# Moving low-part subtractions from DMA to VectorE, and re-spacing background taps, in a one-core hybrid trunk layer

## The chip, the core and the metric

The kernel runs on one core of one Trainium2 chip. The metric is the device time of one execution in microseconds (us). The core's engines run side by side, each through its own list of instructions in a fixed order, and they wait for one another by semaphores: PE (TensorE, the matrix unit; PEld is its weight load), DVE (VectorE), ACT (ScalarE), POOL (GpSimd, which here mostly issues DMAs) and SP (SyncE, which issues the loads and stores).

## The reference, cut to what matters

One layer over 512 prompt tokens and 64 sample tokens (T = 576 in all), model width 1024. A normed input goes through one wide projection and feeds three branches; sigmoid gates merge them, and a last projection closes the layer.

```python
h = _rmsnorm(x, norm_pre_w)
glu_v, glu_g, conv_gate, z, xbc, dt_raw, q, xa_gate, gates = jnp.split(h @ w_in, points, axis=-1)
u = glu_v * jax.nn.sigmoid(glu_g)
c, new_a = _causal_dwconv(u, st_a, conv_dw_w, conv_dw_b)              # width 31
c = jax.nn.silu(_layernorm(c, conv_ln_w, conv_ln_b)) * jax.nn.silu(conv_gate)
out_a = c @ conv_out_w
...                                                                  # y: state-space mixer
out_b = y @ ssd_out_w
...                                                                  # o: attention to 256 memory tokens, 4 heads
out_c = (o * jax.nn.silu(xa_gate)) @ xa_out_w
g = jax.nn.sigmoid(gates + gate_b).reshape(bsz, t, N_BRANCH, D_MODEL)
m = g[:, :, 0] * out_a + g[:, :, 1] * out_b + g[:, :, 2] * out_c
x_new = x + _rmsnorm(m @ w_out, norm_post_w)
```

## The kernel before

**High and low parts.** Matrix products run in a rounded 32-bit format. To keep the precision, each operand is split into a high part (`hi`, a rounded copy made by ACT) and a low part (`lo` = value minus `hi`), and each product is three matmuls: hi·hi, hi·lo, lo·hi. A weight tile's low part is made in one of two ways. Either DVE subtracts (`wlo` at L191, `wlo<-sm` at L920), or ACT writes minus the value into `lo` (L193, L908; in the rounded format this is minus the high part) and POOL issues a DMA that adds the raw weights on top (L194, L909).

**Weights.** `order` is a list of weight jobs; `W(name)` prepares jobs up to two ahead (`prep_to`): SP loads `raw`, ACT writes `whi` (L189), and the low part follows. The buffers `raw`, `whi` and `wlo` have three slots each. `proj` then runs 48 matmuls of 288 columns (24 products in two halves).

**Stages in order of time.** The state-space mixer (to about 460 us); the first GLU tiles and the last four `out_b` products, with the projections `cg0` and `cg1`; the *pair stage* (about 516 to 725 us), in which two output tiles at a time are computed by seven half-size products P1 to P7 instead of eight (a Strassen scheme) for 17 pairs; four attention heads; eight merges of the attention branch (`merge(j, 2, ...)`, products `oc0` to `oc7`); the *late projections* (`cg5`, `cg6`, `g0_0` to `g0_4`, `cg7`, `g0_5` to `g0_7`); the layer norm of the convolution branch; eight merges of that branch (`oa0` to `oa7`); and the output projection.

**The pair stage.** The slots follow the list `seq`: P2 of pair p+1 and P1 of pair p+1 stand among P5, P6, P7, P3, P4 of pair p. P1, P2 and P4 use a weight block as it is (`pair_pure`: `ph` is its high part, `pl` its low part); P5/P6 and P7/P3 use sums of blocks (`pair_sum`: four DVE adds `sm`, two ACT copies `whi`, two DVE subtractions `wlo` per pair). P2 accumulates in a PSUM tile `Z`, P1, P6, P7 and P4 in `X`, P5 and P3 in `Y`. These PSUM tiles take the place of the `mm` tiles of `cg0` and `cg1`: `Z` and `X` of the first pair can only be written once DVE has read `cg0` and `cg1` (L863).

**Background taps.** The width-31 convolution is done by DVE: for each of eight channel tiles, 30 scalar_tensor_tensor instructions (a *tap* each, L791) on 128 x 606 values. The closures wait in a list `bg`; `bgrun(n)` takes the next n from it and gives them a low priority, so that the scheduler puts them behind the other work near that place. After a tile's last tap ACT copies the result back (L798, L799) and DVE adds it to `csum` (L803). The layer norm needs all 240 taps: `csum`, its split `sh`/`sl` (L1305, L1306), four matmuls with a matrix of ones (L1309, L1310, called *ln_sum*), the mean (L1315); then the squares, a second ln_sum, ACT's square root (L1327), a reciprocal (L1328), eight multiplications (L1359), and per channel tile a tanh and four DVE steps, of which the last is the low part at L620. Those eight tiles (`chl`) are the operands of `oa0` to `oa7`.

**What sets the order.** A scheduler fixes each engine's list when the program is built. On the chip each engine works through its list strictly in that order.

Of the kernel before, what the change touches and what calls it, by code (L numbers as in the profile page):

```python
# [8 lines left out]
F32 = mybir.dt.float32  # L9
F32R = mybir.dt.float32r  # L10
AF = mybir.ActivationFunctionType
ALU = mybir.AluOpType
# [3 lines left out]
T = 576  # L16
# [12 lines left out]
def hybrid_trunk_kernel(  # L29
# [9 lines left out]
    nc = tc.nc  # L39
# [129 lines left out]
    nprep = [0]  # L169
    limit = [hold - 1]  # L170

    def prep_to(n):
        while nprep[0] <= min(n, len(order) - 1, limit[0]):
            name, src, c0, r0, kk, cols = order[nprep[0]]
            raw = wp.tile([128, 1024], F32, tag="raw", name="raw", bufs=3)
            hi = wp.tile([128, 1024], F32R, tag="whi", name="whi", bufs=3)
            lo = wp.tile([128, 1024], F32R, tag="wlo", name="wlo", bufs=3) if name != "dt" else hi
            n_ = kk * cols
            nc.sync.dma_start(
                out=raw[:, :n_].rearrange("p (k c) -> p k c", k=kk),  # L180
                in_=src[r0:r0 + 128 * kk, c0:c0 + cols].rearrange("(k p) c -> p k c", p=128),
            )
            if name == "dt":
                w = hi[:, :2 * n_].rearrange("p (k c) -> p k c", k=kk)
                rw, wh, wl = raw[:, :n_].rearrange("p (k c) -> p k c", k=kk), w[:, :, 0:32], w[:, :, 32:64]
                a = nc.scalar.activation(wh, rw, AF.Copy)
                b = nc.vector.tensor_tensor(wl, rw, wh.bitcast(F32), ALU.subtract)
            else:
                a = nc.scalar.activation(hi[:, :n_], raw[:, :n_], AF.Copy)  # L189
                if nprep[0] < pos["gg0"] or name[0] in "kv":  # L190
                    b = nc.vector.tensor_tensor(lo[:, :n_], raw[:, :n_], hi[:, :n_].bitcast(F32), ALU.subtract)  # L191
                else:
                    nc.scalar.activation(lo[:, :n_], raw[:, :n_], AF.Copy, scale=-1.0)  # L193
                    nc.gpsimd.dma_start(out=lo[:, :n_], in_=raw[:, :n_], accum_op=ALU.add)  # L194
            if nprep[0] in (2, 3):
                tc.keep_in_program_order(a)
                tc.keep_in_program_order(b)
            ready[name] = (w, None) if name == "dt" else (
                hi[:, :n_].rearrange("p (k c) -> p k c", k=kk),
                lo[:, :n_].rearrange("p (k c) -> p k c", k=kk),  # L200
            )
            nprep[0] += 1
# [424 lines left out]
    def gating_a(g):  # L627
        ys = [gx[4 * g + j][:, 0:T] for j in range(4)]
        tot = s2.tile([128, T], F32, tag="tot", name="tot", bufs=1)
        for j in range(4):  # L630
            nc.vector.tensor_tensor(ys[j], ys[j], gz[4 * g + j], ALU.mult)
            if j == 0:
                nc.scalar.activation(tot, ys[j], AF.Square)
            else:
                sq = s2.tile([128, T], F32, tag="gsq", name="gsq", bufs=1)
                nc.scalar.activation(sq, ys[j], AF.Square)
                nc.vector.tensor_tensor(tot, tot, sq, ALU.add)
        th = hl[0].tile([128, T], F32R, tag="hi", name="th")
        tl = hl[0].tile([128, T], F32R, tag="lo", name="tl")
        nc.scalar.activation(th, tot, AF.Copy)  # L640
        nc.vector.tensor_tensor(tl, tot, th.bitcast(F32), ALU.subtract)
        gtot[g] = (ys, th, tl)
# [61 lines left out]
    def bgrun(n):  # L704
        with tc.high_priority(offset=-150):
            for _ in range(min(n, len(bg))):
                bg.pop(0)()
# [146 lines left out]
    push_conv(2)  # L854
    for q in range(4):
        out_b(3, q)
        bgrun(4)
    st.close()
    for j in range(2):
        pt = proj(f"cg{j}")  # L860
        t = sx.tile([128, 640], F32, tag="bc", name="bc", bufs=4)[:, 0:T]
        nc.scalar.activation(v2(t), va(pt), AF.Tanh, scale=0.5)
        nc.vector.scalar_tensor_tensor(v2(t), v2(t), 1.0, va(pt), ALU.add, ALU.mult)  # L863
        nc.scalar.dma_start(out=spill["cg"][j], in_=t)
        bgrun(6)

# [34 lines left out]
    def pair_pure(p, w, pr):  # L903
        src = pw[p][w]
        hi = sp.tile([128, 512], F32R, tag="ph", name="ph", bufs=5)
        lo = sp.tile([128, 512], F32R, tag="pl", name="pl", bufs=4)
        nc.scalar.activation(hi, src, AF.Copy)  # L907
        nc.scalar.activation(lo, src, AF.Copy, scale=-1.0)  # L908
        nc.gpsimd.dma_start(out=lo, in_=src, accum_op=ALU.add)  # L909
        pw[p][pr] = hi, lo  # L910

    def pair_sum(p, prs, sums):
# [127 lines left out]
    for i, (p, pr) in enumerate(seq):  # L1040
        if (p, pr) == (7, "P5"):
            mem_load()
        if (p, pr) == (9, "P5"):
            mem_prep()
        while todo and todo[0][0] <= i:
            todo.pop(0)[1]()
        slot(p, pr)
        if (p, pr) == (np_ - 1, "P6"):
            limit[0] = len(order)
            prep_to(hold + LA - 1)  # L1050
        if i % 3:
            bgrun(1)
    stp.close()
    stp = ExitStack()
# [125 lines left out]
    def att_scores(h, khi, klo, qhi, qlo, ckh, ckl):  # L1180
        vv = token_major(None, o_mv, h, v_proj(h))
        vhl = hilo(a1, [128, 2, 256], "vv", vv)
        Ps = []
        for tp in range(3):
            ps = ps_tile()
            cnt = 2 if tp < 2 else 1
            n = 128 if tp < 2 else 64
            for t in range(cnt):
                t0 = 256 * tp + 128 * t
                kh_, kl_ = (khi, klo) if tp < 2 else (ckh, ckl)  # L1190
                mac1(
                    ps[:n, 256 * t:256 * t + 256],
                    [(qhi[:, i, t0:t0 + n], qlo[:, i, t0:t0 + n], kh_[:, i], kl_[:, i]) for i in range(2)],
                )
            Ps.append(softmax(ps, n, cnt))
            bgrun(2)
        return vhl, Ps

    def att_pt(h, Ps):
# [89 lines left out]
    def merge(j, br, gname, oname, act, ob=ob):  # L1289
        if gname is None:  # L1290
            t = sx.tile([128, 640], F32, tag="bc", name="bc", bufs=4)[:, 0:T]
            nc.sync.dma_start(out=t, in_=spill["g2"][j])
        else:
            t = gname
        pt = proj(oname, act=act)
        bgrun(5)
        nc.vector.scalar_tensor_tensor(v2(t), v2(t), 1.0, va(pt), ALU.add, ALU.mult)  # L1297
        nc.vector.tensor_tensor(ob[:, j], ob[:, j], t, ALU.add)

# [38 lines left out]
        else:  # L1338
            g0t.append(gate_t(f"g0_{j}", 0, j, hlA, "lo", 8))

    for j in range(2):
        sgs[j] = hlA.tile([128, T], F32, tag="hi", name="hi", bufs=8)
        nc.sync.dma_start(out=sgs[j], in_=spill["cg"][j])
    for e in late[:2]:
        late_job(*e)
        bgrun(5)
# [1 line left out]
    late_job(*late[2])  # L1348
    late_job(*late[3])
    ln_mean()  # L1350
    for e in late[4:6]:
        late_job(*e)
    late_job(*late[6])
# [156 lines left out]
```

## Time and profile before

| | us |
|---|---|
| three timed runs: median (lowest to highest) | 1122.64 (1122.12 to 1125.76) |
| the profiled execution, its own time | 1124.0 |
| its span, first to last instruction | 1122.3 |
| PE busy in it | 1091.3 |
| DVE busy in it | 852.6 |
| ACT busy in it | 614.7 |
| POOL busy in it | 152.9 |

The profile is of one execution. The span leaves out 1.7 us that lie around the instructions. Busy times overlap. PE is busy for 97% of the span, so about 31 us of it are without a matmul; some 6 us of these lie behind the last matmul.

### The profile page before, as it was taken

How to read it: one execution, taken by the hardware profiler on the slowest of the kernel's cores; microseconds unless marked ns; L12 is line 12 of the kernel's file. 1: busy time of each engine (PE TensorE's matmuls, PEld its weight loads, DVE VectorE, ACT ScalarE, POOL GpSimd, SP SyncE). 2: the span in 40 equal slices, each digit the busy share in tenths (PEclk: the TensorE clock that was granted, in tenths of full speed). 3: DMA queues.
4: the chain of work that ended last, by engine and by line, in shares of the span. 5: the costliest groups of instructions: out<-in, count | busy, mean ns of one | idle time of the engine just before them, and what ended most of it. 6: DMA issues, size and time to landing. Idle time of an engine off the chain costs nothing. (4 is left out here: it accounts for less than half of the span.)

```text
span 1122.3 us, 20511 instructions
## 1 busy us (share of the span) xinstructions
PE 1091.3 (97%) x8081; PEld 1047.8 (93%) x8081; DVE 852.6 (76%) x1353; ACT 614.7 (55%) x1086; POOL 152.9 (14%) x247
## 2 busy tenths in 40 slices
PE   8999999999999999998999999999999999999997
PEld 8999999999999999998999999999999999999974
DVE  5778898578878984698898897669888789575533
ACT  5664675456436543745666656645655633675431
POOL 0100120012002100312323422100000111111000
PEclk9999999999999999998999999999999999999999
DMA  7354433442353235679797698666558698677812
GB/s 208 95 165 118 144 111 103 128 118 80 95 146 96 87 82 131 148 168 211 160 246 175 146 229 211 160 193 171 151 153 198 152 279 199 152 169 177 253 39 84
DMA packets 204086, 172.03 MB, mean 153 GB/s; under 512 B 15222, under 2 KB 176030, under 8 KB 203990
## 3 DMA queue, kind: packets, MB, share of 16 engines
q1 hardware_dynamic: 188006, 128.18, 39.5%
q0 software_dynamic: 14544, 39.59, 19.6%
q10 hardware_dynamic: 1440, 2.95, 0.7%
q8 instruction: 63, 1.03, 0.4%
q14 instruction: 33, 0.27, 0.1%
HBM read 116.49 MB, written 14.62 MB: 117 GB/s over the span
## 5 line engine op out<-in xcount | busy, mean ns | idle before, releaser
L214 PE MATMUL mm<-hT,whi 128*128 128x288 f32 (+2 forms) x2240 | 398.7, 298 | 2.9 <-DVE hi L476 1.3
L214 PEld LDWEIGHTS mm<-hT,whi 128*128 128x128 f32 x2240 | 334.5, 189 | 6.1 <-issue 1.5
L214 PE MATMUL mm<-hT,wlo 128*128 128x288 f32 (+2 forms) x1120 | 247.2, 298 | 0.2 <-DMA wlo<-raw 0.2
L189 ACT ACTIVATE whi<-raw 128x1024 fp32r<-128x1024 f32 x118 | 124.7, 1056 | 200.4 <-PE mm L214 157.6
L791 DVE SCALAR_TENSOR_TENSOR c<-u,dww,c 128x606 f32<-128x606 f32 x240 | 200.4, 844 | 2.5
L214 PEld LDWEIGHTS mm<-hT,wlo 128*128 128x128 f32 x1120 | 185.0, 189 | 1.3 <-issue 0.5
L191 DVE TENSOR_TENSOR wlo<-raw,whi 128x1024 fp32r<-128x1024 f32 x68 | 83.0, 1220 | 43.4 <-ACT whi L189 43.0
L214 PE MATMUL mm<-hi,whi 128*128 128x288 f32 x512 | 111.4, 299 | 0.3 <-DVE lo L1297 0.3
L214 PE MATMUL mm<-lo,whi 128*128 128x288 f32 x512 | 110.6, 296 | 0.0
L214 PE MATMUL mm<-hi,wlo 128*128 128x288 f32 x512 | 110.2, 296 | 0.0
L194 POOL DMA_DIRECT2D wlo<-raw x50 | 43.7, 873 | 396.5 <-ACT wlo L193 311.4
L214 PEld LDWEIGHTS mm<-hi,whi 128*128 128x128 f32 x512 | 82.4, 188 | 1.7 <-issue 1.1
L214 PEld LDWEIGHTS mm<-lo,whi 128*128 128x128 f32 x512 | 82.8, 188 | 0.0
L214 PEld LDWEIGHTS mm<-hi,wlo 128*128 128x128 f32 x512 | 82.7, 188 | 0.0
L193 ACT ACTIVATE wlo<-raw 128x1024 fp32r<-128x1024 f32 x50 | 52.4, 1048 | 16.1 <-PE ps L214 15.1
L466 DVE SCALAR_TENSOR_TENSOR acc<-xp,scw,acc 128x579 f32<-128x579 f32 x72 | 58.3, 813 | 3.1 <-ACT acc L462 1.9
L907 ACT ACTIVATE ph<-rawb 128x512 fp32r<-128x512 f32 x34 | 21.5, 632 | 56.5 <-PE X L937 29.9
L920 DVE TENSOR_TENSOR wlo<-sm,whi 128x1024 fp32r<-128x1024 f32 x34 | 41.4, 1219 | 7.3 <-ACT whi L919 7.3
L458 POOL COPY tails<-xp 128x3 f32<-128x3 f32 x24 | 18.9, 789 | 191.0 <-ACT xp L456 185.9
L919 ACT ACTIVATE whi<-sm 128x1024 fp32r<-128x1024 f32 x34 | 35.9, 1055 | 10.7 <-PE X L937 5.8
L909 POOL DMA_DIRECT2D pl<-rawb x34 | 29.6, 870 | 79.2 <-ACT pl L908 48.5
L937 PE MATMUL X<-hT,ph 128*128 128x288 f32 x136 | 28.7, 304 | 4.2 <-DVE bc L863 4.2
(373 smaller groups left out, 2257.1 us busy)
## 6 DMA issues: line engine op xcount, KB each, us to landing
raw<-in_w_in_dram SPq DMA_DIRECT2D x70, 512.0 KB
wlo<-raw POOLq DMA_DIRECT2D x50, 512.0 KB, 5.4
raw<-in_w_in_dram SPq DMA_DIRECT2D x34, 256.0 KB
rawb<-in_w_in_dram SPq DMA_DIRECT2D x34, 256.0 KB
pl<-rawb POOLq DMA_DIRECT2D x34, 256.0 KB, 4.3
R<-scr SPq DMA_DIRECT2D x16, 512.0 KB
raw<-in_ssd_out_w_dram SPq DMA_DIRECT2D x16, 512.0 KB
raw<-in_xa_kv_w_dram SPq DMA_DIRECT2D x16, 512.0 KB
```

Source lines behind the costliest of these rows:

```text
L189: a = nc.scalar.activation(hi[:, :n_], raw[:, :n_], AF.Copy)
L191: b = nc.vector.tensor_tensor(lo[:, :n_], raw[:, :n_], hi[:, :n_].bitcast(F32), ALU.subtract)
L193: nc.scalar.activation(lo[:, :n_], raw[:, :n_], AF.Copy, scale=-1.0)
L194: nc.gpsimd.dma_start(out=lo[:, :n_], in_=raw[:, :n_], accum_op=ALU.add)
L214: m = nc.tensor.matmul(o, lhsT=w, rhs=r[:, s:s + w_], start=(i == 0 and a == 0), stop=(i == n - 1 and a == 2),)
L466: nc.vector.scalar_tensor_tensor(acc, xp[:, r:r + 579], w4[:, r, jt:jt + 1], acc, ALU.mult, ALU.add)
L791: nc.vector.scalar_tensor_tensor(c, upad[j][:, r:r + NC], w31[:, r, j:j + 1], c, ALU.mult, ALU.add)
L907: nc.scalar.activation(hi, src, AF.Copy)
L909: nc.gpsimd.dma_start(out=lo, in_=src, accum_op=ALU.add)
L919: nc.scalar.activation(hi, sm, AF.Copy)
L920: nc.vector.tensor_tensor(lo, sm, hi.bitcast(F32), ALU.subtract)
L937: nc.tensor.matmul(o, lhsT=w[:, k], rhs=r[:, k], start=(start and k == 0 and a == 0), stop=(k == 3 and a == 2), skip_group_check=True,)
```

## The change

- In the pair stage the low part of P2's block comes from a DVE subtraction, no longer from an ACT copy and an accumulating DMA. P1 and P4 keep the old way.
- The low parts of the weights `oa0` to `oa7` come from DVE too.
- `bgrun` is called for fewer taps ahead of and in the first pairs (3 and not 4 behind each of the four last `out_b`; none behind `cg0` and `cg1`, where it was 6; every second slot for the first 60 slots of `seq`, where it was two slots of three), and for more later (3 and not 2 behind the first two score tiles of each head; 6 and not 5 in each merge).
- In `gating_a` the third square gets a buffer of its own.
- The loads of `cg0` and `cg1` from their spill stand behind `ln_mean()`, no longer ahead of the late projections.

Lines behind the inserted ones move by up to five: L863 becomes L866, L920 becomes L925, L1309 becomes L1314, and so on.

```diff
@@ prep_to
-                if nprep[0] < pos["gg0"] or name[0] in "kv":
+                if nprep[0] < pos["gg0"] or name[0] in "kv" or name[:2] == "oa":
                     b = nc.vector.tensor_tensor(lo[:, :n_], raw[:, :n_], hi[:, :n_].bitcast(F32), ALU.subtract)
                 else:
                     nc.scalar.activation(lo[:, :n_], raw[:, :n_], AF.Copy, scale=-1.0)
@@ gating_a
-                sq = s2.tile([128, T], F32, tag="gsq", name="gsq", bufs=1)
+                if j == 2:
+                    sq = s2.tile([128, T], F32, tag="acc", name="gsq2", bufs=2)
+                else:
+                    sq = s2.tile([128, T], F32, tag="gsq", name="gsq", bufs=1)
@@ last out_b, cg0, cg1
         out_b(3, q)
-        bgrun(4)
+        bgrun(3)
...
         nc.scalar.dma_start(out=spill["cg"][j], in_=t)
-        bgrun(6)
@@ pair_pure
-        nc.scalar.activation(lo, src, AF.Copy, scale=-1.0)
-        nc.gpsimd.dma_start(out=lo, in_=src, accum_op=ALU.add)
+        if pr == "P2":
+            nc.vector.tensor_tensor(lo, src, hi.bitcast(F32), ALU.subtract)
+        else:
+            nc.scalar.activation(lo, src, AF.Copy, scale=-1.0)
+            nc.gpsimd.dma_start(out=lo, in_=src, accum_op=ALU.add)
@@ pair loop
-        if i % 3:
+        if i % (2 if i < 60 else 3):
             bgrun(1)
@@ att_scores
-            bgrun(2)
+            bgrun(3 if tp < 2 else 2)
@@ merge
-        bgrun(5)
+        bgrun(6)
@@ behind the attention merges
-    for j in range(2):
-        sgs[j] = hlA.tile([128, T], F32, tag="hi", name="hi", bufs=8)
-        nc.sync.dma_start(out=sgs[j], in_=spill["cg"][j])
     for e in late[:2]:
         late_job(*e)
         bgrun(5)
@@
     ln_mean()
+    for j in range(2):
+        sgs[j] = hlA.tile([128, T], F32, tag="hi", name="hi", bufs=8)
+        nc.sync.dma_start(out=sgs[j], in_=spill["cg"][j])
```

**Where the order moves, 1: DVE from the first pair's sums to `cg1`.** The rows below are DVE's, from the first pair's sums (`sm`) to the second reading of a `cg` tile (`bc<-bc,mm`); `c<-u` rows are taps. First before, then changed.

```order
L916 TENSOR_TENSOR sm<-sm,rawb 128x512
L920 TENSOR_TENSOR wlo<-sm,whi 128x1024
L863 SCALAR_TENSOR_TENSOR bc<-bc,mm 128x576
L791 SCALAR_TENSOR_TENSOR c<-u,dww,c 128x606 x2
L916 TENSOR_TENSOR sm<-raw,rawb 128x512
L920 TENSOR_TENSOR wlo<-sm,whi 128x1024
L791 SCALAR_TENSOR_TENSOR c<-u,dww,c 128x606 x2
L916 TENSOR_TENSOR sm<-sm,raw 128x512
L863 SCALAR_TENSOR_TENSOR bc<-bc,mm 128x576
```

```order
L925 TENSOR_TENSOR wlo<-sm,whi 128x1024
L866 SCALAR_TENSOR_TENSOR bc<-bc,mm 128x576
L921 TENSOR_TENSOR sm<-raw,rawb 128x512
L925 TENSOR_TENSOR wlo<-sm,whi 128x1024
L921 TENSOR_TENSOR sm<-sm,raw 128x512
L921 TENSOR_TENSOR sm<-raw 128x512
L921 TENSOR_TENSOR sm<-sm,rawb 128x512
L925 TENSOR_TENSOR wlo<-sm,whi 128x1024
L866 SCALAR_TENSOR_TENSOR bc<-bc,mm 128x576
```

The four taps between the two readings are gone; two more sums and the second pair's first subtraction (`wlo`) have moved ahead of the second reading.

**2: DVE from the last taps into the layer norm.** Again DVE's rows, from the end of the convolution (`csum<-csum,u`) to the first steps per tile. Between the split `sl` and the reciprocal the rows of the mean and the squares are the same in both and are left out here, so each list is shown in two pieces. Before:

```order
L476 SCALAR_TENSOR_TENSOR hi<-hi,mm 128x576
L791 SCALAR_TENSOR_TENSOR c<-u_7445,dww,c 128x606 x3
L803 TENSOR_TENSOR csum<-csum,u_7445 128x576
L1306 TENSOR_TENSOR sl<-csum,sh 128x576
```

```order
L1328 RECIPROCAL mean<-mean 128x576
L1359 TENSOR_TENSOR u<-u,mean 128x576 x7
L1359 TENSOR_TENSOR u_7445<-u_7445,mean 128x576
L476 SCALAR_TENSOR_TENSOR hi<-hi,mm 128x576
L1363 TENSOR_SCALAR u<-u,vecs 128x576 x2
L1364 SCALAR_TENSOR_TENSOR u<-th,u 128x576 x2
```

Changed:

```order
L476 SCALAR_TENSOR_TENSOR hi<-hi,mm 128x576
L794 SCALAR_TENSOR_TENSOR c<-u_7403,dww,c 128x606
L806 TENSOR_TENSOR csum<-csum,u 128x576
L794 SCALAR_TENSOR_TENSOR c<-u_7403,dww,c 128x606 x15
L806 TENSOR_TENSOR csum<-csum,u_7403 128x576
L1311 TENSOR_TENSOR sl<-csum,sh 128x576
```

```order
L191 TENSOR_TENSOR wlo<-raw,whi 128x1024
L1333 RECIPROCAL mean<-mean 128x576
L1364 TENSOR_TENSOR u<-u,mean 128x576 x7
L1364 TENSOR_TENSOR u_7403<-u_7403,mean 128x576
L191 TENSOR_TENSOR wlo<-raw,whi 128x1024
L1368 TENSOR_SCALAR u<-u,vecs 128x576 x2
L191 TENSOR_TENSOR wlo<-raw,whi 128x1024
L1369 SCALAR_TENSOR_TENSOR u<-th,u 128x576 x2
```

Counted over DVE's whole list, 30 taps are left at the last attention merge's reading (L1302) where 14 were left at L1297 before, and three low parts of `oa` weights (L191) now stand between the second ln_sum and the first tile; a reading of a projection (L476) has left that place.

**3: PE at the first ln_sum.** PE's rows (with tile numbers): `mm_11248` is the projection `g0_1` before, `mm_11389` is `g0_3` in the changed program; `ps<-sh` and `ps<-sl` are the sums. Before, then changed.

```order
L214 MATMUL mm_11248<-hT0_92,wlo_11119 128x288 x2
L1309 MATMUL ps_11302<-sh_11298,onesr_77 128x288
L1309 MATMUL ps_11303<-sh_11298,onesr_77 128x288
L214 MATMUL mm_11348<-hT0_92,whi_11184 128x288
L1310 MATMUL ps_11302<-sl_11299,onesr_77 128x288
```

```order
L214 MATMUL mm_11389<-hT0_92,wlo_11222 128x288 x2
L214 MATMUL mm_11447<-hT0_92,whi_11325 128x288 x2
L1314 MATMUL ps_11281<-sh_11277,onesr_77 128x288
L1314 MATMUL ps_11282<-sh_11277,onesr_77 128x288
L214 MATMUL mm_11447<-hT1_93,whi_11325 128x288 x2
```

Both programs have 7754 matmuls. The first ln_sum has moved back by two projections: it is number 6915 of PE's list and was number 6817. The second is number 7071 and was 6976. The first matmul of `oa0` is number 7161 in both.

## The prediction

> **What bounds the kernel now.** I read the page first, then the windows by stage, then PE's waits.
>
> ```profile
> span 1122.3 us, 20511 instructions
> PE 1091.3 (97%) x8081; PEld 1047.8 (93%) x8081; DVE 852.6 (76%) x1353; ACT 614.7 (55%) x1086; POOL 152.9 (14%) x247
> ...
> L791 DVE SCALAR_TENSOR_TENSOR c<-u,dww,c 128x606 f32<-128x606 f32 x240 | 200.4, 844 | 2.5
> ```
>
> PE is the bound: the change takes no matmul away, so it can only win idle PE time or time at a low clock. The windows say where that is (span, busy time with count per engine, granted clock, DMA).
>
> ```profile
> 0.00:500.00 500.00, 494.41 (x3796) 473.09 (x3797) 386.81 (x665) 278.27 (x511) 63.64 (x148) 1.00 0.46 123
> 500.00:530.00 30.00, 25.24 (x171) 24.77 (x170) 23.35 (x32) 12.15 (x21) 5.16 (x6) 0.89 0.89 203
> 530.00:730.00 200.00, 191.96 (x1415) 189.10 (x1414) 170.42 (x253) 131.16 (x233) 52.70 (x57) 0.99 0.80 190
> 730.00:940.00 210.00, 205.92 (x1569) 201.10 (x1568) 172.97 (x260) 107.80 (x197) 16.44 (x19) 1.00 0.73 188
> 940.00:1025.00 85.00, 83.60 (x626) 83.13 (x624) 58.37 (x80) 52.80 (x70) 10.59 (x12) 1.00 0.72 164
> 1025.00:1122.00 97.00, 90.14 (x514) 76.56 (x514) 40.69 (x67) 32.48 (x58) 4.34 (x5) 0.98 0.47 133
> ```
>
> PE idles 4.8 us around the first pair, 8.0 in the other pairs, 4.1 in the heads and attention merges, and only 1.4 from there to 1025. In that last stretch DVE has 85 - 58 = 27 us free. PE's waits name the releasers (total, times, longest):
>
> ```profile
> PE Z L937 <- DMA pl<-rawb: 5.0, 4, 1.6
> PE X L937 <- DVE bc L863: 4.2, 1, 4.2
> ...
> PE mm L214 <- DVE hi L476: 1.3, 1, 1.3
> ...
> PE Z L937 <- DVE bc L863: 0.6, 1, 0.6
> ```
>
> So the change aims at 5.0 + 4.2 + 0.6 us of waits. What follows a wait costs too: the clock. These are windows along its steps.
>
> ```profile
> 517.49:520.90 3.41, 0.76 (x6) 0.53 (x5) 3.41 (x5) 0.00 (x0) 0.00 (x0) 1.00 0.85 246
> 520.90:524.30 3.40, 1.84 (x8) 1.85 (x8) 3.40 (x6) 2.47 (x4) 0.00 (x0) 0.50 0.28 89
> 524.30:527.73 3.43, 3.43 (x16) 3.43 (x16) 3.43 (x6) 1.18 (x3) 1.53 (x2) 0.50 0.98 227
> 606.24:609.65 3.41, 1.74 (x12) 1.27 (x10) 3.41 (x7) 2.91 (x5) 0.32 (x1) 1.00 0.74 123
> 609.65:613.06 3.41, 3.25 (x13) 3.25 (x14) 3.38 (x6) 0.00 (x0) 1.42 (x1) 0.50 1.05 272
> 694.98:698.40 3.42, 2.28 (x17) 2.28 (x18) 3.42 (x6) 0.79 (x2) 0.00 (x0) 1.00 0.77 240
> 698.40:701.80 3.40, 3.40 (x28) 3.40 (x27) 0.31 (x1) 2.97 (x6) 1.68 (x2) 1.00 0.44 76
> ```
>
> A window with PE 22%, 54% or 51% busy is followed by one at clock 0.50; a window 67% busy is not. A wait of 1.5 to 2 us inside one window therefore costs another 1.7.
>
> **Term 1, the first pair: -1.9 us.** P1's PSUM tile is free once DVE has read `cg1` (the second L863). DVE and PE there:
>
> ```profile
> 515.61 0.75 DVE L863 SCALAR_TENSOR_TENSOR bc<-bc,mm 128x576 f32<-128x576 f32 x1
> ...
> 517.79 0.68 DVE L916 TENSOR_TENSOR sm<-raw,rawb 128x512 f32<-128x512 f32 x1
> 518.40 1.22 DVE L920 TENSOR_TENSOR wlo<-sm,whi 128x1024 fp32r<-128x1024 f32 x1
> ...
> 521.65 0.75 DVE L863 SCALAR_TENSOR_TENSOR bc<-bc,mm 128x576 f32<-128x576 f32 x1
> ...
> 522.46 0.85 PE L937 MATMUL X<-hT,ph 128*128 128x288 f32 x2 [4.20 <-DVE bc L863]
> ```
>
> Four taps go from between the two readings, but by the changed order two more sums and the second pair's `wlo` come in, and on ACT the high part that this `wlo` needs (1.06 us, the L189 row below) now stands ahead of `cg1`'s tanh. The taps dropped ahead of the first reading were run while loads were awaited; ACT has two copies less there, so I put the first reading's end at 515.7 instead of 516.3. From there (steps from start to start: `sm` 0.6, `wlo` 1.15): `sm` 516.3, `wlo` 517.4, `sm` 518.0, ACT's high part 519.1, `wlo` 520.3, reading 521.0, P1 at 521.1: 1.4 us earlier. In the half-rate windows 24 matmuls took 5.3 us; at 0.133 us each (18.80 / 141, below) they need 3.2, so 2.1 were lost. From 521.1 one half-rate window to 524.3 loses 1.6. Gain 1.4 + 0.5. Bounds: 0 (ACT later still) to 7 (the waits and their clock all gone).
>
> **Term 2, the other pairs: -6.9 us.** P2's accumulate goes. By the order its replacement on DVE stands behind P3 of the pair three before, 11 slots of 12 matmuls ahead of its use, 11 x 12 x 0.133 = 17 us, so the four waits (5.0) go. The clock of 0.99 over 200 us is the one half-rate window, behind such a wait: 3.4 x 0.5 = 1.7. I add 0.2 for ACT, which drops 17 copies. What is late next? P1's and P4's accumulates, but their queue gets shorter. DVE gains 17 x 0.68 = 11.6 us, but by the order 24 fewer taps (24 x 0.84 = 20) run before the pairs end, so its 170 of 200 us do not grow. Bounds: 2 (most of the waits return as waits for DVE) to 9 (ACT's waits shrink too).
>
> A rule speaks against the 1.7. The Trainium skill (TensorE: Matmul & The Clock Gate, "Part 1: The HAM clock gate") has the clock drop after at least one idle window of about 3.4 us. By it waits of 1.5 us cost no clock, and the time would be 1.7 higher, 1125.0. The row at 606.24, half busy and followed by 0.50, disagrees; I go by the row.
>
> **Term 3, the layer norm: +9.5 us.** The taps not run early are run late: 30 are left at the last attention merge, by the order, against 14. DVE's and PE's rows with the chain of waits:
>
> ```profile
> 957.51 0.76 DVE L803 TENSOR_TENSOR csum<-csum,u 128x576 f32<-128x576 f32 x1 [0.84 <-ACT u L799]
> 961.39 0.76 DVE L1306 TENSOR_TENSOR sl<-csum,sh 128x576 fp32r<-128x576 f32 x1 [3.12 <-ACT sh L1305]
> ...
> 964.56 0.43 PE L1309 MATMUL ps<-sh,onesr 128*128 128x288 f32 x2
> ...
> 965.39 18.80 PE mm L214 x141
> 984.21 1.06 ACT whi L189
> ...
> 986.67 0.42 PE L1310 MATMUL ps<-sl,onesr 128*128 128x288 f32 x2
> ...
> 988.16 0.90 ACT mean L1327 x2
> 989.08 3.76 DVE mean L1328
> ...
> 998.31 0.68 DVE hi L476
> ...
> 1019.53 0.76 DVE L620 SCALAR_TENSOR_TENSOR lo<-hi 128x576 fp32r<-128x576 f32 x1 [0.75 <-ACT hi L616]
> ...
> 1024.44 0.43 PE L214 MATMUL mm<-hi,wlo 128*128 128x288 f32 x2
> ```
>
> 16 more taps x 0.84 = 13.4 put `sl` at 962.2 + 13.4 = 975.6. PE comes to the first ln_sum 98 matmuls later, 964.56 + 13.0 = 977.6, and does not wait, by 2 us. The second ends 95 matmuls (12.6) later, at 987.1 + 12.6 = 999.7. ACT's square root stood behind other copies (988.16); now it can follow at once, 999.9 to 1000.8, so the reciprocal starts 11.7 later than 989.08. Of three `oa` low parts one hides ahead of the reciprocal, two lie in DVE's chain (2 x 1.2 = 2.4); a reading has left it (-0.7), and ACT's dropped copies give back its waits (-1.0). The last low part ends at 1020.3 + 11.7 + 2.4 - 0.7 - 1.0 = 1032.7; PE's last 12 matmuls of `oa0` and `oa1` take 1.6: 1034.3, where it was 1024.9. PE's cover is gone: between second sum and `oa0` it has 81 matmuls (10.8 us) left, where it had 176 (23.4). Its gap of some 6 us there brings half-rate windows, but DVE sets the pace. Bounds: 6 (both low parts hidden) to 14 (2 us of DVE lag and a low clock at the end).
>
> **Costed at nothing:** the square's buffer (PE has no wait at those sums), the later `cg` loads (read only in the layer norm, 50 us behind their issue), the later `oa` low parts (DVE is busy 41 of the last 97 us), and the taps added to the heads and merges: eight each, 13 us of DVE beside its 37 free us. Together -1 to +2, from PE's 4.1 us of idle time there.
>
> **Sum:** 1124.0 - 1.9 - 6.9 + 9.5 = 1124.7 for the profiled execution's own time. That lies 1.4 above the median of the runs, so 1123.3. A measurement of this kernel tells some 0.3%, 3.4 us, from no change.
>
> **The rivals.**
> - *Faster: the first gap closes.* If DVE reads `cg1` as soon as its tanh is done, all 7 of term 1 go, and ACT's waits in the pairs shrink (term 2 at 8.5): 1122.6 - 7 - 8.5 + 9.5 = 1116.6. For it: DVE releases that wait, and taps go. Against it: ACT's high part ahead of the tanh. 0.20.
> - *Slower: DVE late at the first ln_sum.* It has 2 us to spare. If the heads' and merges' extra taps, or taps that follow one another in one tile (15 of the 30 do), cost DVE over 2 us more, PE stands still there too, one for one: with 5 us beyond the point, 1123.3 + 5 = 1128.3. For it: DVE is 82% busy in that stage. Against it: DVE waits for a load early in the merges, and PE is held nowhere there now. 0.18.
> - *It does not do what it says: P2 still waits*, for its loads or for DVE, and term 2 is nothing: 1130.2. Against it: the releaser in all four waits is the accumulate. 0.05.
> - *The page's rule holds:* 1125.0, by trading 1.7 of term 2. 0.02.
>
> **How the numbers follow.** My forecast, a near draw of two gains against one loss, has 0.55. With the page's rule, within 0.3% has 0.57; faster by more 0.20; slower by more 0.23. The range takes in most of both sides and the bounds of terms 1 to 3, which will not all fall one way: 1117 to 1128.5.
>
> **What would show it.** Right: PE's waits for `pl` in `Z` gone; a wait of 3 to 4 us at P1 of the first pair, still for DVE's `bc`; a new PE gap of 5 us or more just ahead of `oa0`, released by DVE or ACT, at about 1002 to 1008; clock 1.00 from 600 to 625. Wrong: PE without a gap ahead of `oa0` (then the kernel is some 9 us faster), or PE waiting at the first ln_sum (slower).

## The result, and the profile after

The changed kernel took 1134.61 us (median of 4 runs, 1133.35 to 1138.47) against 1122.66 for the kernel before beside it (4 runs, 1122.12 to 1125.76): a ratio of 1.0106, 95% interval 1.0076 to 1.0137. It is slower by about 12 us, where no change was forecast. The profiled execution took 1134.62, so its trace speaks for the median; it stands 10.6 us above the profile of before.

The head of the page of the changed kernel, then its windows at about the same places of the program as those of before (columns as there; the counts show that some rows differ by up to 30 matmuls):

```profile
span 1132.9 us, 20473 instructions
...
PE 1093.7 (97%) x8081; PEld 1048.5 (93%) x8081; DVE 871.9 (77%) x1378; ACT 600.7 (53%) x1061; POOL 125.6 (11%) x222
```

```profile
0.00:504.00 504.00, 492.88 (x3781) 470.79 (x3782) 383.17 (x660) 277.14 (x511) 57.76 (x147) 1.00 0.45 122
504.00:536.00 32.00, 28.33 (x201) 28.03 (x201) 20.43 (x29) 12.50 (x21) 4.26 (x5) 0.95 0.79 191
536.00:728.00 192.00, 187.09 (x1392) 184.62 (x1391) 168.40 (x251) 121.97 (x214) 39.35 (x43) 1.00 0.71 175
728.00:941.00 213.00, 208.74 (x1579) 203.62 (x1578) 179.14 (x271) 109.72 (x198) 16.44 (x19) 0.99 0.71 183
941.00:1036.00 95.00, 86.70 (x624) 85.13 (x623) 75.10 (x100) 51.47 (x69) 7.81 (x9) 0.96 0.58 137
```

PE's matmul records are 8081 in both pages. (The order lists count 7754; the distances of 98 and 95 matmuls that the prediction uses come out of the trace as well.) PE's idle time fell from 8.0 to 4.9 us in the other pairs, rose from 1.4 to 8.3 in the stretch of the layer norm (with a clock of 0.96), and rose in the first row, the mixer, where nothing was forecast: 5.6 us in 500 before, 11.1 in 504 now. PE's waits of the changed kernel (total, times, longest) name the releasers:

```profile
PE mm L214 <- ACT hi L616: 5.9, 1, 5.9
PE mm L214 <- DVE sz L476: 4.8, 3, 2.6
PE X L942 <- DVE bc L866: 3.7, 1, 3.7
PE ps L1182 <- ACT pts L1226: 3.6, 3, 1.5
PE mm L214 <- DVE lo L620: 2.1, 2, 1.5
...
PE Y L942 <- ACT whi L924: 1.5, 2, 0.7
PE X L942 <- ACT u L1003: 1.1, 2, 0.6
PE Z L942 <- DVE pl L911: 1.0, 1, 1.0
```

The wait of `Z` for the accumulating DMA is gone; 1.0 us at `Z` is now a wait for DVE's subtraction. New are the waits ahead of `oa0` (`hi` and `lo`, 8.0 us). Much longer are those for `sz`, the mixer's gate tiles; in the same view of before their row read:

```profile
PE mm L214 <- DVE sz L476: 0.7, 2, 0.5
```

For the rest of the document the time is placed with five instructions that both kernels have. Each number is the start of that instruction in one kernel's profile less its start in the profile of before, so the difference of two neighbouring columns is what the stage between them cost. It is one execution of each kernel, and the spread of the runs (last section) goes into every row.

| kernel | last `out_b` (503) | 2nd pair's P1 read (539) | last P7 (723) | last attention merge (940) | first `oa` merge (1024) | span |
|---|---|---|---|---|---|---|
| changed | +6.0 | +2.0 | -1.1 | +0.8 | +10.6 | +10.6 |
| square back | 0.0 | -2.4 | -5.0 | -4.7 | +5.1 | +5.1 |
| square alone | +7.4 | +7.6 | +7.2 | +9.1 | +9.3 | +9.3 |
| square in a buffer of its own | +5.3 | +4.4 | +9.6 | +10.2 | +10.9 | +10.9 |
| taps alone | +1.1 | -5.6 | -9.6 | -8.6 | -0.7 | -0.7 |
| P2 by DVE alone | -0.4 | -0.2 | -5.5 | -6.1 | -5.5 | -5.5 |
| all low parts, old taps, old square | -0.5 | +0.1 | -5.2 | -5.8 | -5.7 | -5.7 |
| first two P2 by DMA | -0.2 | -5.6 | -7.8 | -4.4 | +5.6 | +5.5 |
| the same, stores later | 0.0 | -4.7 | -6.7 | -6.6 | +3.6 | +3.6 |
| mixed version | -0.7 | -7.2 | -7.6 | -4.2 | -3.4 | -3.4 |
| taps later | -0.3 | -5.2 | -1.4 | -0.7 | -0.2 | -0.2 |
| taps later, P2 of pairs 9 to 16 | +1.2 | -5.5 | -7.1 | -7.9 | -7.1 | -6.8 |
| mixed, taps later | +1.6 | -3.4 | -2.4 | -1.4 | -2.5 | -2.5 |

The first row is the result taken apart: +6.0 in the mixer, -4.0 around the first pair, -3.1 in the other pairs, +1.9 in heads and attention merges, +9.8 in the layer norm.

### The profile page after: what moved, and what is told of

Its sections match the earlier page's. It is cut to its first block, busy times and chain, and to the rows that moved or that the text cites. A ratio compares the mean times of both kernels' runs of the same rounds, so it can differ in the third digit from the quotient of the medians.

```text
span 1132.9 us, 20473 instructions
## 1 busy us (share of the span) xinstructions
PE 1093.7 (97%) x8081; PEld 1048.5 (93%) x8081; DVE 871.9 (77%) x1378; ACT 600.7 (53%) x1061; POOL 125.6 (11%) x222
## 4 chain that ended last, share of the span: by engine, by line
PE 56%; DVE 5%; DMA 3%; ACT 2%; issue 1%; POOL 0%; DVEq 0%; SPq 0%; ACTq 0%; POOLq 0%
PE mm L214 27%; PE X L942 9%; PE Y L942 5%; PE ps L214 4%; PE ps L1157 2%; PE Z L942 2%; PE ps L1156 2%; PE ps L1158 2%; DMA wlo<-raw 1%; DMA rawb<-in_w_in_dram 1%; DVE c L794 1%; PE ps L1453 1%; DVE wlo L191 1%; PE ps L599 0%; DMA ob<-msc 0%
## 5 line engine op out<-in xcount | busy, mean ns | idle before, releaser
L191 DVE TENSOR_TENSOR wlo<-raw,whi 128x1024 fp32r<-128x1024 f32 x76 | 92.8, 1221 | 45.4 <-ACT whi L189 45.1
L194 POOL DMA_DIRECT2D wlo<-raw x42 | 36.6, 871 | 349.2 <-ACT wlo L193 302.8
L193 ACT ACTIVATE wlo<-raw 128x1024 fp32r<-128x1024 f32 x42 | 44.1, 1049 | 23.0 <-PE ps L214 20.7
L925 DVE TENSOR_TENSOR wlo<-sm,whi 128x1024 fp32r<-128x1024 f32 x34 | 41.5, 1221 | 8.0 <-ACT whi L924 8.0
L458 POOL COPY tails<-xp 128x3 f32<-128x3 f32 x24 | 15.6, 652 | 189.8 <-ACT xp L456 184.2
L559 ACT ACTIVATE M<-R,tok 128x128 f32<-128x128 f32 (+1 forms) x80 | 24.7, 379 | 9.9 <-PE ps L599 9.9
```

Of the source, the lines that this page charges most:

```text
L559: nc.scalar.activation(M[:, 4 + e, :], R[:nl, 4 + e, :], AF.Relu, scale=-1.0, bias=tok[:nl, 0, c, a + 4:a + 5])
L925: nc.vector.tensor_tensor(lo, sm, hi.bitcast(F32), ALU.subtract)
```

## The experiments

Each kernel was timed beside runs of the kernel before on the same chip (medians of those 1123.8 to 1124.8 us), and its ratio is to these. All compute the whole reference.

**The square back** (the changed kernel, third square in its old buffer):

```diff
-                if j == 2:
-                    sq = s2.tile([128, T], F32, tag="acc", name="gsq2", bufs=2)
-                else:
-                    sq = s2.tile([128, T], F32, tag="gsq", name="gsq", bufs=1)
+                sq = s2.tile([128, T], F32, tag="gsq", name="gsq", bufs=1)
```

> The changed kernel, with the third square of gating_a back in its old buffer; all else as changed. Theory: the square's new buffer is what put PE some 6 us late by the first pair (the second cg reading at 526.3 instead of 521.7), so this one comes in at 1134.6 - 6 = 1128.6 us, with PE in the mixer stage as before (1.5 us or less of waits for DVE's sz where the change had 4.8) and the gap of about 6 us ahead of oa0 still there. Rival: the 6 us come from somewhere else (loads, the scheduler's view of later work): then 1133 to 1135 us.

Measured: 1129.03 us (1127.07 to 1132.25), ratio 1.0042 (1.0024 to 1.0060). As expected: the mixer's +6.0 is gone, and the gap ahead of `oa0` is still there (5.9 us).

**The square alone** (the kernel before, with that edit the other way):

> The kernel before, with only the third square in the acc buffer. Theory: 1122.7 + 6 = 1128.7 us, PE's waits for DVE's sz at about 162, 276 and 387 us as in the change, and everything behind them late by about 6 us. Rival: a later stage takes it up (the convolution taps get 6 us more time): 1123 to 1125 us.

Measured: 1132.33 us (1131.07 to 1136.9), ratio 1.0071 (1.0043 to 1.0100). One edit that was costed at nothing makes about two thirds of the loss. Each kernel against the kernel before beside it: the change costs 12.0 us, with the square back 4.3, so 7.7 go with it; alone it costs 7.6, more than the 6 expected. (The profiles have +6.0 and +7.4 in the mixer, and the intervals leave some 2 to 4 us either way.) Nothing takes it up later. Of the 6.0 us in the changed kernel's mixer, PE's waits for `sz` make 4.1 (4.8 against 0.7), in three places at 162, 276 and 387 us. The longest is followed here. ACT's rows at 262 to 272 us, of the changed kernel and then of before (`sz` is the tanh that DVE needs to read a projection's bank and so to free it for PE, `hi` a copy of the gated rows):

```profile
262.12 0.91 ACT L462 ACTIVATE acc<-xp,half,scw 128x579 f32<-128x579 f32 x1
266.71 0.69 ACT L616 ACTIVATE hi<-xs 128x576 fp32r<-128x576 f32 x1 [3.69 <-DVE xs L677]
...
267.61 1.98 ACT L616 ACTIVATE hi<-xs 128x576 fp32r<-128x576 f32 x3
269.49 1.04 ACT L189 ACTIVATE whi<-raw 128x1024 fp32r<-128x1024 f32 x1
270.56 1.28 ACT L475 ACT_TABLE_LOAD   x1
271.85 0.65 ACT L475 ACTIVATE sz<-mm 128x576 f32<-128x576 f32 x1
```

```profile
259.48 0.89 ACT L462 ACTIVATE acc<-xp,half,scw 128x579 f32<-128x579 f32 x1
260.39 1.28 ACT L467 ACT_TABLE_LOAD   x1
261.69 0.69 ACT L467 ACTIVATE xp<-acc 128x579 f32<-128x579 f32 x1
...
263.39 1.41 ACT L616 ACTIVATE hi<-xs 128x576 fp32r<-128x576 f32 x2 [0.53 <-DVE xs L674]
264.71 1.04 ACT L189 ACTIVATE whi<-raw 128x1024 fp32r<-128x1024 f32 x1
265.66 0.67 ACT L616 ACTIVATE hi<-xs 128x576 fp32r<-128x576 f32 x1
266.24 0.63 ACT L475 ACTIVATE sz<-mm 128x576 f32<-128x576 f32 x1
```

Before, a tanh of the convolution (`xp`) brought the table of tanh back ahead of the copies; now that tanh stands behind `sz`, the table is loaded after all four `hi`, and `sz` comes 5.6 us later, of which 2.6 are there at `acc` already. In the changed order ACT stands idle for 3.69 us ahead of the first `hi`, until DVE's `xs` is done; before, the table load and the tanh filled that time, and 0.53 us of idleness was left. PE pays for it (the timeline of the changed kernel):

```profile
275.88 0.77 PE L214 MATMUL mm<-hT,whi 128*128 128x288 f32 x4 [2.64 <-DVE sz L476]
```

**A buffer of its own.** My theory was that the edit puts the square into one of the two slots through which conv4's accumulators (`acc`) go, and so holds these up. To take the sharing away, the kernel before got

```diff
+                if j == 2:
+                    sq = s2.tile([128, T], F32, tag="gsq2", name="gsq2", bufs=1)
+                else:
+                    sq = s2.tile([128, T], F32, tag="gsq", name="gsq", bufs=1)
```

> The kernel before with the third square in a buffer of its own (a new tag, one slot), neither the old shared one nor conv4's ring. Theory: what costs is the shared ring: the square takes one of the two slots through which conv4's accumulators go, DVE's and ACT's order around 262 to 276 us shifts and the sz gates come late. With a slot of its own the time is that of before, 1122.7 (1121 to 1125), and the last out_b stands within 1.5 us of before. Rival: it is the square's place in the engines' order (it may start before the second sum) that costs, whatever buffer it has: about 1132 as with the ring, the last out_b 6 to 7 us late.

Measured: 1130.5 us (1128.89 to 1134.91), ratio 1.0073 (1.0048 to 1.0099). The theory fell: with no sharing the loss is the same within the intervals, and the same wait stands at the same place:

```profile
275.43 0.77 PE L214 MATMUL mm<-hT,whi 128*128 128x288 f32 x2 [1.90 <-DVE sz L476]
```

What the two versions share is that the third square no longer waits until the second has been added to the sum. The scheduler then places the squares, the root and all that follows differently on ACT, DVE and PE, and the new order is worse. Which of the moved rows is to blame beyond `sz` was not taken apart. (The profiled execution of this kernel took 1134.91 us, 4.4 above the median; its table row has 5.2 us in the other pairs, with three half-rate windows where the square alone has one.)

**The taps alone** (the kernel before with the five changed tap numbers):

> The kernel before, with only the numbers of taps per bgrun changed: low parts, square and spill loads as before. By the order the first ln_sum stands at PE's matmul 6915, as in the change, and 29 taps are left at the last attention merge. Theory (late taps make the layer norm's loss): a PE gap of 4 to 6 us ahead of oa0, the layer norm 8 us worse, the first pair 0 to 2 us better: 1128 to 1131 us. Rival (the oa low parts in DVE's chain make it): no gap over 2 us ahead of oa0, 1121 to 1124 us.

Measured: 1126.03 us (1121.94 to 1128.89), ratio 1.0007 (0.9986 to 1.0028). The gap ahead of `oa0` came as expected, and without any low part of `oa` by DVE: from the last attention merge to `oa0` it loses 7.9 us (-8.6 to -0.7). Missed was the gain ahead of it: 5.6 us at the second pair, where 0 to 2 were expected, and 4.0 more up to the last P7. (The profiled execution took 1123.35 us, 2.7 under the median, so not all of that gain is in the runs.) Its waits:

```profile
PE mm L214 <- ACT hi L616: 4.5, 1, 4.5
...
PE Z L936 <- DMA pl<-rawb: 2.4, 2, 1.5
PE Z L936 <- DVE bc L863: 2.4, 1, 2.4
```

Fewer taps halve the waits for the accumulating DMA by themselves, and at the first pair `X` does not wait at all; 2.4 us are left, at `Z`, with no half-rate window.

**P2 by DVE alone, and all low parts with the old taps.** The first has one edit over the kernel before:

```diff
-        nc.scalar.activation(lo, src, AF.Copy, scale=-1.0)
-        nc.gpsimd.dma_start(out=lo, in_=src, accum_op=ALU.add)
+        if pr == "P2":
+            nc.vector.tensor_tensor(lo, src, hi.bitcast(F32), ALU.subtract)
+        else:
+            nc.scalar.activation(lo, src, AF.Copy, scale=-1.0)
+            nc.gpsimd.dma_start(out=lo, in_=src, accum_op=ALU.add)
```

> The kernel before with one edit: P2's low parts are subtracted by DVE. Theory: these waits are worth what the trace of before showed behind Z, 5.0 us of waits from 540 us on, and in the first pair nothing, since X there waits behind the same reading of cg1; so 1122.7 - 5 = about 1117.5 (1116 to 1119.5), merge 0 in the trace about 5.5 us earlier than before, and the 3.4 us window at half rate in the first pair still there. Rival: out_a's low parts by DVE bring part of what the kernel with all three low-part edits and the old taps gained; then this kernel stands 2 us above that one's 1119.6, at 1120.5 to 1122.

> The changed kernel, with the old numbers of taps per bgrun: low parts by DVE, square and later spill loads stay. Theory: no gap ahead of oa0 over 2 us (first ln_sum at PE's matmul 6817), the square's +6, the pairs' gain of 5 to 7 for P2: 1122 to 1125 us. Rival (the oa low parts make the layer norm's loss): a gap of 5 us or more stays there, 1129 to 1134 us.

The second expectation says that the square's edit stays; the kernel that ran has the square in its old buffer, so it shows the low parts and the later spill loads only. Measured: P2 alone 1121.43 us (1117.52 to 1122.79), ratio 0.9980 (0.9963 to 0.9996); with `oa` by DVE and the spill loads too 1119.56 us (1118.34 to 1122.73), ratio 0.9961 (0.9943 to 0.9980). P2 alone lies where its rival had it, at 1120.5 to 1122, and not at the 1116 to 1119.5 expected. But the intervals of the two ratios overlap, and in the table the two are alike within 0.4 us. P2 gains 5.3 us in the pairs there; whether `oa` by DVE and the later loads gain 1 or 2 us beside it is not shown, and no loss is seen. Neither has a gap ahead of `oa0`.

**The first two pairs' P2 by DMA** (the kernel with the square back, and in `pair_pure`):

```diff
-        if pr == "P2":
+        if pr == "P2" and p > 1:
```

> The changed kernel with the square back in its old buffer, and P2's low parts of the first two pairs by ACT and a DMA again; later pairs by DVE. Theory: in the first pair the DVE's subtraction keeps ACT and DVE on pair 1's low part while cg1's bank is read, so X waits 3.7 us and the clock falls to half for 3.4 us; without it the first pair goes as with the taps alone, where X does not wait and no window is at half rate: 3 to 5 us less than with only the square back, 1124 to 1126, and no half-rate window between 515 and 535. Rival: the first pair's X wait has another cause (the later pairs' order): 1129, X wait of 3 us or more still there.

Measured: 1129.57 us (1125.28 to 1131.07), ratio 1.0046 (1.0019 to 1.0073). The mechanism showed itself, the time did not. ACT's rows at the first pair with the square back (`bc<-mm` is the tanh of `cg0`, then of `cg1`), and with this kernel:

```profile
514.06 0.62 ACT L862 ACTIVATE bc<-mm 128x576 f32<-128x576 f32 x1
514.59 1.04 ACT L921 ACTIVATE whi<-sm 128x1024 fp32r<-128x1024 f32 x1
...
518.53 1.06 ACT L921 ACTIVATE whi<-sm 128x1024 fp32r<-128x1024 f32 x1 [2.90 <-DVE sm L918]
519.50 0.63 ACT L862 ACTIVATE bc<-mm 128x576 f32<-128x576 f32 x1
```

```profile
514.98 1.33 ACT L862 ACTIVATE bc<-mm 128x576 f32<-128x576 f32 x2
...
517.93 0.51 PE L939 MATMUL Z<-hT,ph 128*128 128x288 f32 x2 [2.31 <-DVE bc L863]
```

With DVE's subtraction in the first pairs, two sums' high parts stand between the two tanhs, the second of them waits for DVE's sums, and `X` waits 3.7 us; without it the tanhs stand together and only `Z` waits. That is worth 3.2 us at the second pair (-5.6 against -2.4; one half-rate window behind the wait for `Z` was not expected). But two waits in the heads then fell so that half-rate windows followed, at 771 and 809 us, and by the last attention merge nothing was left (-4.4 against -4.7).

**The stores later.** That kernel still lost 6.1 us between the second pair and the eighth, whose P1 is read at 608 us in the profile of before (-5.6 to +0.5). SP's stores of `ob` stood between the halves of a weight load there, so I wrote them five slots later:

```diff
-            nc.sync.dma_start(out=msc[j], in_=ob[:, j])
+            held.append((now[0] + 5, j))
...
+        now[0] = i
+        while held and held[0][0] <= i:
+            j_ = held.pop(0)[1]
+            nc.sync.dma_start(out=msc[j_], in_=ob[:, j_])
         slot(p, pr)
```

> The kernel with the first two pairs' P2 by ACT and a DMA (square in its old buffer, the rest as in the change), and the stores of out_a's first gated rows (msc from ob, for pairs 1 to 4) written five slots later in the code, so that in SP's list no store stands between the two halves of a weight load. Theory: these stores wait for DVE's ob 13 us in all from 555 to 600 there (4.5 before the change) and hold the loads behind them; ACT's copy of the late half (6.1 us of wait for rawb) then holds the copy out of the X bank, so PE waits 1.7 us at X and 1.0 at Z. With the stores later, ACT's wait for rawb falls under 3 us, X's wait for ACT's ct there under 0.5, and the eighth pair's c1 stands 2 to 4 us earlier against before than its +0.5. Rival: the loads wait for their buffers' last readers and not for the stores: ACT's wait for rawb stays at 5 us or more and the eighth pair's c1 within 1 us of +0.5.

Measured: 1128.25 us (1126.17 to 1130.1), ratio 1.0034 (1.0017 to 1.0051). The theory fell. The eighth pair stood at +1.5, and ACT's wait for the load and PE's for the copy behind it stayed. The last row is SP's, of 570 to 576 us:

```profile
ACT ph L906 <- DMA rawb<-in_w_in_dram: 6.2, 1, 6.2
...
PE X L939 <- ACT ct L1010: 1.8, 1, 1.8
```

```profile
SPq L896 <- DMA pl<-rawb: 3.9, 1, 3.9
```

The load was issued at 574.68, as soon as an accumulate that reads its buffer had landed; before the stores were moved the same wait (4.2 us) had held it until 574.00. So the accumulate held it, as the rival has it, and not a store. With the taps alone a load waits 4.8 us there in the same way, and yet ACT's wait for it is 1.9 us. Why it is 6.2 here stays open.

**A mixed version**: square old, P2 by DVE from the third pair on, `oa` and the spill loads old, fewer taps at the first pair, 16 given back in the pairs' second half and in the heads (three in each tile). Against the changed kernel, besides `p > 1` as above:

```diff
-        if i % (2 if i < 60 else 3):
+        if i % (3 if i < 60 else 4):
...
-            bgrun(3 if tp < 2 else 2)
+            bgrun(3)
```

> A version from the parts that gained: the square in its old buffer, P2's low parts by DVE from the third pair on only, fewer taps ahead of the first pair as in the change, and the 16 taps given back in the later pairs and in the attention heads, so that as many are left at the merges as before (50 and 14); out_a's low parts and the spill loads as before. Theory: the first pair gains the 5.6 us that the taps alone showed there, the later pairs some 4 us, and the layer norm loses nothing: 1122.7 - 9.6 = 1113 (1111 to 1116). Rival: the taps given back in the pairs and heads put DVE on their chain, or the two gains are the same waits: no better than the kernel with the old taps, 1119 to 1121.

Measured: 1119.83 us (1117.15 to 1123.75), ratio 0.9968 (0.9950 to 0.9985), in the rival's range and not at 1113. The gains do add up to the last P7 (-7.6) and the layer norm costs 0.9 us, but 3.4 go from there to the last attention merge, with two half-rate windows in the heads (772 and 810 us).

**Taps later, three ways.** First the changed tap numbers with the 16 taps given back in the pairs' second half alone:

```diff
-        if i % (2 if i < 60 else 3):
+        if i % (2 if i < 60 else 99):
...
-        pt = proj(oname, act=act)
-        bgrun(6)
+        pt = proj(oname, act=act)
+        bgrun(5)
```

> The kernel before with tap numbers alone: fewer around the first pair and in the first half of the pairs as in the change, three in the first tiles of the heads as in the change, but one in every slot of the pairs' second half, and five in the merges as before, so that as many taps are left at the merges as before (49 and 14). Theory: the gap ahead of out_a's first block is a matter of the taps that are left at the merges, since the layer norm's sum comes only behind the last of them; with 49 and 14 it stays shut, and the 9.4 us that the taps alone gained up to the merges reach the end: 1122.7 - 9.4 = 1113.3 (1111 to 1116), nothing above 1.5 us ahead of out_a's first block. Rival: the taps in the pairs' second half make DVE late there, as it is busy 77% of that stretch before: X and Z wait for DVE and 3 to 6 us of the gain go, 1117 to 1119.

> The same tap numbers, and P2's low parts by DVE from the tenth pair on (pairs 9 to 16), by ACT and a DMA before. Theory: the tenth pair on holds most of the waits of Z that the trace of before shows (0.5, 1.5, 1.6 us), and DVE has room: about 2 us below the same tap numbers with the old way, 1111 to 1113. Rival: with few taps ahead the DMA's low parts are on time anyway, or DVE's subtraction only puts other DVE work back: no difference within 1 us, or up to 2 us above it.

> The mixed version with its taps moved: P2's low parts by DVE from the third pair on, fewer taps ahead of the first pair, two taps in every tile of the heads as before, one in every slot of the pairs' second half (47 left at the first merge). Theory: the mixed version lost its gain in the heads, where three taps put 1.4 us of waits for DVE's ptl beside those for ACT's pts and the clock fell to half in two windows; with two taps no window there, and the 7.6 us of the pairs reach the end: 1122.7 - 7.5 = 1115 (1113 to 1117). Rival: the half-rate windows in the heads fall by where the waits lie against the clock's windows, whatever the taps: one or two are still there, and 1118 to 1120 again.

Measured: 1124.15 us (1122.81 to 1125.88), ratio 1.0000 (0.9987 to 1.0013); with P2 by DVE in pairs 9 to 16 1120.14 us (1117.24 to 1122.36), ratio 0.9958 (0.9938 to 0.9978); the mixed version with its taps there 1120.42 us (1118.57 to 1122.17), ratio 0.9967 (0.9952 to 0.9983). All three lie 5 us or more above the times expected, 1113, 1112 and 1115. In all three no gap stands ahead of `oa0`, as expected. In the first the gain was lost in the very pairs that got the taps (-5.2 to -1.4), but not to waits for DVE:

```profile
PE Z L936 <- DMA pl<-rawb: 5.8, 4, 2.9
```

With P2 by DVE in those pairs that row is 1.0, the page of the execution reads

```profile
span 1115.5 us, 20515 instructions
...
PE 1088.1 (98%) x8081; PEld 1044.4 (94%) x8081; DVE 858.2 (77%) x1361; ACT 612.4 (55%) x1078; POOL 143.5 (13%) x239
```

and no window from 60 to 1100 us is at half rate. (It took 1117.24 us, 2.9 under the median.) It and the old-tap kernel with all low parts take some 0.4% less than the kernel before, the least of all that ran; the intervals do not tell them from each other or from the two mixed versions. The third lost in the pairs (-3.4, then +4.1 at the eighth), its heads without a half-rate window.

## Why the prediction was wrong

By its own sum the profiled execution should have stood 0.7 us above before; it stood at 10.6. The 9.9 us between come from five terms:

- **"Costed at nothing: the square's buffer (PE has no wait at those sums)": the step that failed, 6.0 us.** The reason was true of the sums and did not bear on the cost. I showed no order for this place and read none: the edit takes away a wait on ACT, and the whole stretch behind it is ordered anew. Undone, it gives back 7.7 us of the runs' medians (1134.61 - 1122.66 against 1129.03 - 1124.76); alone, it costs 7.6 (1132.33 - 1124.76).
- **Term 2, the other pairs: -6.9 forecast, -3.1 measured, the second miss.** With the square back, the profile still stands 5.1 us above before where the sum says 0.7; this term, -2.6 there, makes 4.3 of those 4.4. The mechanism was right: the waits for the accumulate went, and the half-rate window between 600 and 625 with them. With the old taps P2 alone gave -5.3, near the forecast. Mis-sized is its sum with the taps: these alone cut the same waits (5.0 to 2.4 us, and 4.0 us of time there), and together the edits brought more waits for ACT and DVE: the rows above show 1.5, 1.1 and 1.0 us, where the same views of before had 0.4, 0.5 and none.
- **Term 1, the first pair: -1.9 forecast, -4.0 measured** (-2.4 with the square back). The wait for `bc` stayed, 3.7 us, within the 3 to 4 foretold; the changed kernel had one half-rate window behind it, the one with the square back two, which makes 1.7 us between them and is chance as far as the forecast goes. The rival that this gap closes was not far: the taps alone do it, and P2's own edit undoes it.
- **Heads and merges: 0 taken (-1 to +2 given), +1.9 measured.** PE's waits there are the same in total, 4.1 us before and 4.2 now. What is new is one half-rate window at 813.75, behind one in which PE was 56% busy: 3.4 x 0.5 = 1.7 us. With the square back no such window fell, and the stage cost 0.3.
- **Term 3, the layer norm: +9.5 forecast, +9.8 measured: right, step by step.** The reciprocal came 11.6 us later counted from the last attention merge (11.7 foretold), PE did not wait at the first ln_sum, and its gap ahead of `oa0` was there, with windows at half rate behind it. It lies at 1011 to 1017 and not at 1002 to 1008, since the stages ahead stood at +0.8 where terms 1 and 2 had -8.8:

```profile
1001.52 3.75 DVE L1333 RECIPROCAL mean<-mean 128x576 f32<-128x576 f32 x1 [1.61 <-ACT mean L1332]
...
1017.01 1.33 PE L214 MATMUL mm<-hi,whi 128*128 128x288 f32 x4 [5.87 <-ACT hi L616]
```

```profile
1011.73:1015.14 3.41, 0.00 (x0) 0.00 (x0) 3.41 (x6) 1.25 (x3) 0.00 (x0) 1.00 0.73 225
1015.14:1018.55 3.41, 1.50 (x5) 1.15 (x6) 3.41 (x7) 2.39 (x4) 0.00 (x0) 0.50 0.56 160
```

Its cause is shown too. By the order of the built programs, the changed tap numbers leave 67 taps at the first attention merge and 29 or 30 at the last, and every such kernel loses 7.9 to 10.1 us from there to `oa0`; the kernels with 47 to 50 left at the first merge lose at most 0.9. Of the 9.8, at most some 2 are the two `oa` low parts (9.7 with the square back, 7.9 with the taps alone, which lack P2's edit and the later loads as well).

Of the rivals none came true. DVE was not late at the first ln_sum; the kernel is slower for a reason that was not on the list.

## What to carry to other kernels

Where a scheduler orders the work, an edit that only removes a wait still has to be read in the order of every engine behind it, and above all where an edit looks too small to cost anything. Edits that aim at the same wait do not add: price each against the kernel that has the others. Work that is put off must have a stage with room ahead of the next point that needs all of it; here some 16 taps more at the last merge cost 8 to 10 us in the layer norm, where kernels that had run them earlier lost at most 0.9.

## What the runs showed of the hardware

**A wait's price depends on where it falls.** The granted clock changes only on a grid of 3.41 us, in all traces. The wait for `sz` was nearly the same with the square alone (2.59 us) and in the changed kernel (2.64), but lay in one window there and across two here:

```profile
272.68:276.09 3.41, 0.82 (x7) 0.61 (x6) 3.41 (x5) 1.98 (x4) 0.00 (x0) 1.00 0.00 1
276.09:279.50 3.41, 3.41 (x16) 3.41 (x15) 3.41 (x6) 0.69 (x1) 1.04 (x2) 0.50 0.46 153
```

```profile
271.03:274.45 3.42, 2.21 (x17) 1.97 (x15) 3.42 (x6) 3.41 (x6) 0.00 (x0) 1.00 0.00 0
274.45:277.86 3.41, 1.98 (x15) 2.01 (x16) 3.41 (x6) 0.28 (x1) 1.03 (x2) 1.00 0.45 136
277.86:281.27 3.41, 3.41 (x28) 3.41 (x27) 3.02 (x5) 0.69 (x1) 0.23 (x2) 1.00 0.23 47
```

PE is 24% busy in the one window and the next runs at half rate (16 matmul records in a full window, not 28); 65% and 58% in the two others, and the clock stays. By the starts of the same PE matmuls against before, the stretch from 265 to 288 us cost 4.0 us there and 2.4 here. Counted over all fourteen profiles from 60 to 1100 us: after a full-rate window in which PE was less than 45% busy the clock always fell (20 times), between 45 and 62% it fell 12 times and stayed 24 times, above that it never fell.

The Trainium skill (TensorE: Matmul & The Clock Gate, "Part 1: The HAM clock gate") asks for at least one idle window before the clock drops; these traces disagree, with drops behind windows that were up to 62% busy.

**The spread of the runs goes with the clock.** A shift by part of a window moves a wait from one window into two. Of the 83 runs of the kernel before beside these experiments, the 22 with a granted clock of 0.997 or more took 1121.8 us on average, the 20 with 0.993 or less 1126.2. The mean clocks of these two groups, 0.997 and 0.993, differ by 0.0043, or 4.8 of 1122 us, near the 4.4 us between them. Where the windows lay in each run is not on record, so that their place makes the difference is argued and not shown. In any case one profile out of such a spread places a cause but does not give the ratio: P2 alone was 5.5 us shorter in its profile and 2.4 in the median.
